# Handing out the recurrences of the first stage: after the ninth projection unit, with RG-LRU one block later and each third's chained parts inside its own group

## The chip, the cores and the metric

The kernel runs on one core of one Trainium2 chip. The metric is the device time of one execution in microseconds, the median of several runs. Three runs of the kernel before gave 2967.48, 2968.40 and 2978.37 us.

## What is computed

One layer of a streaming encoder over T = 2064 tokens (2048 and 16 learned ones in front), width 1024, in float32. Three head groups read one normalised input through one combined projection; their outputs go through one output projection, and a gated feed-forward part follows.

```python
p = rms_norm(h, norm_mix_pre[l]) @ w_in[l]                   # 1024 -> 3080 columns
oa = rg_lru_group(xa, ya, ...)                               # p[:512]: conv, gates, linear recurrence
ob = forgetting_attention_group(q, k, v, f_logit, f_bias)    # p[512:2056]: 8 heads, causal, decay by cumsum(log f)
oc = rwkv7_group(pc, ...)                                    # p[2056:]: 4 heads, 64 x 64 state per head
mixed = jnp.concatenate([oa, ob, oc], axis=-1) @ w_out[l]
h = h + rms_norm(mixed, norm_mix_post[l])
f = causal_dwconv(rms_norm(h, norm_ffn_pre[l]) @ ffn_up[l], ffn_conv[l])
gate, val = jnp.split(f, 2, axis=-1)
h = h + rms_norm((jax.nn.gelu(gate) * val) @ ffn_down[l], norm_ffn_post[l])

def step(S, inp):                                            # the RWKV recurrence, over all tokens
    s_kk = einsum('bhij,bhj->bhi', S, kk_t)
    S = S * w_t[:, :, None, :] - s_kk[..., None] * (kk_t * a_t)[:, :, None, :] + v_t[..., None] * k_t[:, :, None, :]
    return S, einsum('bhij,bhj->bhi', S, r_t)
```

## The kernel before

The program has stages: input projection with the two recurrent groups beside it, attention, output projection, feed-forward up and down. The change is in the first stage only.

**Input projection.** The tokens are worked through in three "thirds" (`part` 0, 1, 2), each of two token blocks (400 and 384, then 384 and 384, then 256 and 256 tokens). For a third, `w_in_part` (L307) is a generator over 25 units, each of 128 output columns: first the gate unit of the attention (`w_in_gate`), then eight units c0 to c7 (the RWKV columns), four a0 to a3 (the RG-LRU columns), and k0 to k3, v0 to v3, q0 to q3. It yields after every unit and token block, in all 50 times for a third, with True where a unit is whole; the last two units, q2 and q3, are interleaved by token block. A unit's matmuls (L177 to L179, PSUM tile `psp`) split each product in three for precision. Columns c and a are stored to a scratch tensor in DRAM (`scr_p`), from which the recurrences load them.

**Recurrences.** RWKV is cut into nine blocks of 256 tokens (the last has 64), three to a third. `Rwkv.block(b)` (L1047) is a generator. Its first part mixes neighbouring tokens, computes decays and gates (matmuls into the one-buffer PSUM tile `eps`, L1075 the first of them), the scores inside a chunk of 64 tokens (L1149, L1154), transposes (L1185), and inverts small triangular matrices on VectorE and GpSimd (L1204, L1205), by way of two DRAM tensors `da` and `dx`; it has four plain yields and then yields `SOLVED`. Its second part ("chained part", ten yields) multiplies the inverses together (L1234, L1278, L1289), carries the 64 x 64 states from chunk to chunk and block to block (L1330, L1334), normalises, and stores to `scr_mix` (L1390 is its last matmul before the store). Its matmuls go to the PSUM tile `rps`, which has two buffers, handed round in program order. `lru_block` (L1453, four yields) does one block of RG-LRU; its state goes from block to block too. `gate_block` (two calls a third) sums the forget gates for attention.

**The order.** `recurrences` (L2113) chains these generators for a third. Per block: the first part up to `SOLVED`; then `R.ending`, which is the chained part of the block before; then this block's RG-LRU. Its own chained part becomes `R.ending` and so comes behind the next block's first part, for the last block of a third in the next third's group, for the very last in the loop behind `beside.finish()`. `Beside` (L2083) holds such groups in a queue and hands out one piece (from one yield to the next) at a time: `advance` is called at every yield of the projection and adds `PACE` = 1.25 to what is due, as long as there is a group; a group begins only when the one before it is at its end. A third's group is added when the unit numbered `READY + 1` = 14 is whole, that is k0, in every third; in the first third the units up to 13 are handed out before the loop begins. What is left after the last third is handed out by `beside.finish()` without projection steps between.

The order in which the program hands out its instructions is a priority: the builder (`schedule_with_timeline_sim=True`) fills each engine's queue, and among instructions that could go at a moment the one handed out earlier goes first. Each engine then works through its queue in that order. Buffers of a tag are handed round in program order.

**Behind it.** The recurrences' pools (`rec`: `ps_rw`, `ps_ae`, `gp`, `rp`) are closed; attention (`Attn.run`) goes through 8 heads with the first half of the queries (two blocks of 512), then 8 heads with the second half. Each of these 32 steps ends with one L761. Some attention tiles (the third key tile `k2_2`, prepared by L499) lie on the side of the memory on which the recurrences' pools were. Only when the first half is through does the output projection begin to run beside attention.

## Time and profile before

| | us |
|---|---|
| median of three runs | 2968.4 |
| the profiled execution | 2975.7 |
| its span, first to last instruction | 2974.0 |
| TensorE matmul busy in the span | 2852.4 (96%) |
| VectorE busy | 2039.5 (69%) |
| ScalarE busy | 1503.8 (51%) |
| GpSimd busy | 1285.9 (43%) |
| mean granted TensorE clock | 0.979 |

The profile is of one execution. The page gives busy times, the span in 40 slices, the DMA queues and the chain of work that ended last; the trace behind it can be asked for the busy time in any stretch, for waits, for groups of instructions by line, and for the instructions in order of time. Times in the trace are counted from the first instruction. "PE" is TensorE's matmuls, "PEld" its weight loads, "DVE" VectorE, "ACT" ScalarE, "POOL" GpSimd, "SP" SyncE, which issues nearly all DMAs. A matmul's end is modelled, so small gaps between matmuls do not show as idle time.

### The profile page before, as it was taken

How to read it: one execution, taken by the hardware profiler on the slowest of the kernel's cores; microseconds unless marked ns; L12 is line 12 of the kernel's file. 1: busy time of each engine (PE TensorE's matmuls, PEld its weight loads, DVE VectorE, ACT ScalarE, POOL GpSimd, SP SyncE). 2: the span in 40 equal slices, each digit the busy share in tenths (PEclk: the TensorE clock that was granted, in tenths of full speed). 3: DMA queues.
4: the chain of work that ended last, by engine and by line, in shares of the span. 5: the costliest groups of instructions: out<-in, count | busy, mean ns of one | idle time of the engine just before them, and what ended most of it. 6: DMA issues, size and time to landing. Idle time of an engine off the chain costs nothing.

```text
span 2974.0 us, 53306 instructions
## 1 busy us (share of the span) xinstructions
PE 2852.4 (96%) x18826; PEld 2444.3 (82%) x18826; DVE 2039.5 (69%) x3977; ACT 1503.8 (51%) x2937; POOL 1285.9 (43%) x1555
## 2 busy tenths in 40 slices
PE   6999999999988889999999999999999999999998
PEld 6998899888866555666568999999999999787887
DVE  5257754665677775566656998888778787646766
ACT  4246432554346655455644665666565665324333
POOL 1001121132114566667722667455655444646443
PEclk9999899999988999999999999999999999999999
DMA  6776479576653358445245665577777764436453
GB/s 216 237 231 220 144 250 320 182 245 218 217 125 81 88 116 229 106 98 136 64 130 189 203 193 175 165 230 211 208 211 219 218 198 138 150 114 221 146 173 121
DMA packets 470344, 530.52 MB, mean 178 GB/s; under 512 B 86862, under 2 KB 356888, under 8 KB 468524
## 3 DMA queue, kind: packets, MB, share of 16 engines
q1 hardware_dynamic: 469308, 526.18, 58.8%
q8 instruction: 148, 2.42, 0.3%
q14 instruction: 120, 0.98, 0.1%
q0 software_dynamic: 768, 0.93, 0.1%
HBM read 368.07 MB, written 158.90 MB: 177 GB/s over the span
## 4 chain that ended last, share of the span: by engine, by line
PE 75%; DVE 8%; DMA 7%; ACT 4%; issue 2%; POOL 2%; SPq 1%; DVEq 0%; POOLq 0%; ACTq 0%
PE psu L177 9%; PE psu L178 9%; PE psu L179 9%; PE psp L179 4%; PE psp L178 4%; PE psp L177 4%; PE psd L177 4%; PE psd L178 4%; PE psd L179 4%; PE po L727 4%; PE pswo L177 2%; PE pswo L178 2%; PE pswo L179 2%; PE sc L704 2%; PE mx L576 2%
## 5 line engine op out<-in xcount | busy, mean ns | idle before, releaser
L178 PE MATMUL psu<-xo,uw 128*128 128x344 f32 x1848 | 591.5, 320 | 0.0
L177 PE MATMUL psu<-xo,uw 128*128 128x344 f32 x1848 | 586.2, 322 | 2.4 <-DVE vb L1889 1.9
L179 PE MATMUL psu<-xo,uw 128*128 128x344 f32 x1848 | 582.0, 320 | 0.3 <-DVE uw L1698 0.3
L177 PE MATMUL psp<-xh,wh 128*128 128x384 f32 (+2 forms) x1152 | 378.7, 329 | 1.4 <-DMA wh<-scr_wk 1.0
L179 PE MATMUL psp<-xh,wl 128*128 128x384 f32 (+2 forms) x1152 | 376.8, 328 | 0.6 <-DMA wl<-scr_wk 0.6
L178 PE MATMUL psp<-xl,wh 128*128 128x384 f32 (+2 forms) x1152 | 375.3, 326 | 0.0
L1698 DVE TENSOR_TENSOR uw<-uq,uw 128x512 fp32r<-128x512 f32 x341 | 320.2, 944 | 59.1 <-ACT uw L1697 55.9
L177 PEld LDWEIGHTS psu<-xo,uw 128*128 128x128 f32 x1848 | 345.9, 188 | 4.2 <-DVE vb L1889 3.0
L178 PEld LDWEIGHTS psu<-xo,uw 128*128 128x128 f32 x1848 | 347.2, 188 | 0.0
L179 PEld LDWEIGHTS psu<-xo,uw 128*128 128x128 f32 x1848 | 345.7, 188 | 1.1 <-DVE uw L1698 1.1
L1697 ACT ACTIVATE uw<-uq 128x512 fp32r<-128x512 f32 x462 | 288.1, 627 | 94.8 <-PE psu L179 44.9
L709 ACT ACTIVATE p<-sc,bias 128x512 f32<-128x512 f32 (+4 forms) x352 | 197.5, 589 | 172.1 <-PE sc L705 142.1
L581 DVE TENSOR_REDUCE mc<-mx 128x1 f32<-128x512 f32 (+6 forms) x352 | 190.7, 567 | 116.7 <-PE mx L576 77.5
L1837 DVE SCALAR_TENSOR_TENSOR uy<-psu,ffn_cols,uy 128x342 f32<-128x342 f32 (+1 forms) x390 | 220.9, 568 | 60.3 <-ACT uy L1835 58.6
L1845 POOL TENSOR_TENSOR uy<-uy,uy 128x342 f32<-128x342 f32 (+1 forms) x132 | 145.1, 1099 | 232.5 <-DVE uy L1837 61.0
L1698 POOL TENSOR_TENSOR uw<-uq,uw 128x512 fp32r<-128x512 f32 x121 | 183.1, 1513 | 133.3 <-ACT uw L1697 111.9
L179 PEld LDWEIGHTS psp<-xh,wl 128*128 128x128 f32 x1152 | 218.6, 190 | 8.9 <-issue 6.2
L177 PEld LDWEIGHTS psp<-xh,wh 128*128 128x128 f32 x1152 | 218.4, 190 | 8.4 <-issue 4.4
L178 PEld LDWEIGHTS psp<-xl,wh 128*128 128x128 f32 x1152 | 218.3, 189 | 7.2 <-issue 5.7
L748 POOL TENSOR_TENSOR acc<-acc,p 128x512 f32<-128x512 f32 (+3 forms) x186 | 198.8, 1071 | 46.8 <-ACT p L709 21.3
L1698 DVE TENSOR_TENSOR fo<-u,fo 128x896 fp32r<-128x896 f32 x88 | 101.6, 1154 | 130.9 <-ACT fo L1697 130.3
L1697 ACT ACTIVATE fo<-u 128x896 fp32r<-128x896 f32 x88 | 81.3, 923 | 207.1 <-PE psd L179 116.0
(490 smaller groups left out, 6339.4 us busy)
## 6 DMA issues: line engine op xcount, KB each, us to landing
uq<-scr_us SPq DMA_DIRECT2D x220, 256.0 KB
uq<-in_ffn_up_dram SPq DMA_DIRECT2D x209, 256.0 KB
wl<-scr_wk SPq DMA_DIRECT2D x48, 512.0 KB
wh<-scr_wk SPq DMA_DIRECT2D x48, 512.0 KB
u<-scr_ff SPq DMA_DIRECT2D x88, 256.0 KB
scr_ff<-uy SPq DMA_DIRECT2D x110, 171.0 KB
raw<-in_w_in_dram SPq DMA_DIRECT2D x24, 512.0 KB
scr_wk<-wh SPq DMA_DIRECT2D x24, 512.0 KB
```

Of the source, the lines that this page charges most:

```text
L177: nc.tensor.matmul(out, ah, bh, start=first, stop=False, skip_group_check=more)
L178: nc.tensor.matmul(out, ah, bl, start=False, stop=False, skip_group_check=more)
L179: nc.tensor.matmul(out, al, bh, start=False, stop=last, skip_group_check=more)
L576: nc.tensor.matmul(ps[:rows, : e - a], q3[:, qo : qo + rows], k2[:, a:e], start=True, stop=not last)
L581: self.reduced = nc.vector.tensor_reduce(mc[:rows, i, ci : ci + 1], ps[:rows, : e - a], axis=AX.X, op=ALU.max)
L709: last = nc.scalar.activation(p[:rows, :w], ps[:rows, :w], AF.Exp, bias=bias[:rows, j : j + 1])
L727: mm = nc.tensor.matmul(po[at : at + 64, c0:n], v1[:rows, j], p[:rows, : n - c0], start=start and i < 2, stop=end and i + 2 >= len(group), ...
L748: eng.tensor_tensor(a, ps_[0][0][:rows, c0:n] if start and i == 1 else a, p[:rows, : n - c0], op=ALU.add)
L1697: core.nc.scalar.activation(hi, src, AF.Copy)
L1698: (eng or core.nc.vector).tensor_tensor(lo, src, hi, op=ALU.subtract)
L1837: core.conved = stt(y[:, :n], src[:, i : n + i], cw[:, 44 * i + cc : 44 * i + cc + 1], y[:, :n], op0=ALU.mult, op1=ALU.add)
L1845: core.pooled = nc.gpsimd.tensor_tensor(v[:, :n], g[:, :n], v[:, :n], op=ALU.mult)
```

## The change

Three things move in program order; no instruction is added or removed.

1. In the second and third thirds the group is added when unit 9 (`ROWS`: the gate unit and c0 to c7) is whole instead of unit 14. The first third is unchanged: k0.
2. A block's RG-LRU comes one block later: behind the first part of the next block, just ahead of the block's own chained part. Before an RG-LRU, pieces are passed over while unit 13 (`READY`) of this third is not whole yet (`R.made`).
3. The chained part of a third's last block, and its RG-LRU, stand at the end of this third's own group instead of inside the next third's, and the loop over `R.ending` behind `beside.finish()` is gone.

```diff
-READY = 13
+READY, ROWS = 13, 9
...
-    for b in ((0, 1, 2), (3, 4, 5), (6, 7, 8))[part]:
+    def rest(b):
+        while R.made < (part, READY):
+            yield
+        yield from lru_block(core, R, scr, lk, b)
+        yield from R.ending
+
+    bs = ((0, 1, 2), (3, 4, 5), (6, 7, 8))[part]
+    for b in bs:
         gen = R.block(b)
         while next(gen) != R.SOLVED:
             yield
-        yield from R.ending
+        if b > bs[0]:
+            yield from rest(b - 1)
         R.ending = gen
-        yield from lru_block(core, R, scr, lk, b)
+    yield from rest(bs[-1])
...
                 for whole in units:
-                    if whole and i == READY + 1:
+                    if whole:
+                        R.made = part, i
+                    if whole and i == (ROWS if part else READY + 1):
                         beside.add(recurrences(core, R, lk, a["fox_f_bias"], scr, blocks, part))
                     beside.advance()
...
         beside.finish()
-        for _ in R.ending:
-            pass
         rec.close()
```

So the order of one third is, before: gates; first part b, chained part b-1, RG-LRU b; first part b+1, chained part b, RG-LRU b+1; and so on. After: gates; first parts b and b+1; RG-LRU b, chained part b; first part b+2; RG-LRU b+1, chained part b+1; RG-LRU b+2, chained part b+2.

## The prediction

> **What bounds the kernel now.** The page first: its engine line, the slices and the chain that ended last.
>
> ```profile
> PE 2852.4 (96%) x18826; PEld 2444.3 (82%) x18826; DVE 2039.5 (69%) x3977; ACT 1503.8 (51%) x2937; POOL 1285.9 (43%) x1555
> PE   6999999999988889999999999999999999999998
> PEclk9999899999988999999999999999999999999999
> PE 75%; DVE 8%; DMA 7%; ACT 4%; issue 2%; POOL 2%; SPq 1%; DVEq 0%; POOLq 0%; ACTq 0%
> ```
>
> TensorE is the bound nearly everywhere. Only slices 12 to 15 (a slice is 2974.0 / 40 = 74.4 us, so 818 to 1115 us) have it below nine tenths, with a lower granted clock in two of them. So the second view is the busy time by stretch, around that place:
>
> ```profile
> core 0: us, PE busy (x) PEld busy (x) DVE busy (x) ACT busy (x) POOL busy (x), PEclk, DMA share, GB/s
> 440.00:500.00 60.00, 59.34 (x361) 55.97 (x358) 26.25 (x60) 17.53 (x37) 10.82 (x14) 1.00 0.93 315
> 700.00:855.00 155.00, 148.95 (x1725) 136.17 (x1726) 101.57 (x279) 80.51 (x172) 31.23 (x57) 0.99 0.61 192
> 855.00:875.00 20.00, 11.76 (x99) 8.29 (x98) 17.58 (x46) 2.59 (x8) 0.59 (x2) 0.71 0.44 113
> 875.00:920.00 45.00, 40.48 (x262) 28.18 (x262) 34.13 (x92) 25.22 (x57) 14.05 (x24) 0.75 0.70 149
> 920.00:1040.00 120.00, 104.61 (x1262) 70.78 (x1261) 93.46 (x276) 73.39 (x165) 67.76 (x115) 0.89 0.33 79
> 1040.00:1080.00 40.00, 36.85 (x285) 22.48 (x284) 30.37 (x76) 23.74 (x53) 26.16 (x39) 1.00 0.53 128
> 1080.00:1120.00 40.00, 31.31 (x142) 18.36 (x143) 27.73 (x76) 18.45 (x38) 25.60 (x37) 0.87 0.50 112
> 855.00:1136.00 281.00, 238.28 (x2116) 155.21 (x2115) 211.22 (x578) 152.08 (x335) 142.81 (x229) 0.87 0.47 108
> 1200.00:1400.00 200.00, 198.36 (x907) 127.47 (x905) 118.09 (x249) 100.50 (x187) 134.72 (x193) 0.99 0.44 106
> ```
>
> The projections keep TensorE full (148.95 of 155 us), and so does attention once the output projection fills its holes (198.36 of 200). Between them, 855 to 1136 us, stands the "bridge": 281.00 - 238.28 = 42.7 us of idle TensorE. What fills the bridge is told by the third view, instructions in order of time:
>
> ```profile
> 565.47 0.70 PE L1075 MATMUL eps<-rwwa,wa_up 64*128 64x256 f32 x2
> 613.71 0.39 PE L296 MATMUL psf<-xh,fw 128*128 128x256 f32 x1
> 766.91 1.13 PE L1075 MATMUL eps<-rwwa,wa_up 64*128 64x256 f32 x4
> 833.12 1.13 PE L1075 MATMUL eps<-rwwa,wa_up 64*128 64x256 f32 x4
> 847.73 1.15 PE L1278 MATMUL rps<-rww,rwsc 64*64 64x64 f32 x32
> 855.24 0.28 PE L179 MATMUL psp<-xh,wl 128*128 128x256 f32 x1
> 926.74 0.66 PE L1075 MATMUL eps<-rwwa,wa_up 64*128 64x64 f32 x4
> 1034.18 0.59 ACT L761 ACTIVATE oh<-po 64x512 f32<-64x512 f32 x1
> 1091.89 0.43 PE L1390 MATMUL rps<-rwsg,g_up 128*128 128x64 f32 x2
> 1102.38 0.59 ACT L761 ACTIVATE oh<-po 64x512 f32<-64x512 f32 x1
> 1135.62 0.60 ACT L761 ACTIVATE oh<-po 64x512 f32<-64x512 f32 x1 [1.89 <-PE po L727]
> ```
>
> The last projection matmul is at 855.24. RWKV still runs: block 5's chained part has just begun (L1278, 847.73), block 7's first part too (L1075, 833.12), block 8 starts at 926.74, and the last block ends at 1091.89. The first half of attention (16 steps, each ended by an L761) ends at 1135.62. How much RWKV and RG-LRU matmul lies on either side of 855, by their two PSUM tiles (rps first, then eps):
>
> ```profile
> 100.00:855.00 755.00, 143.49 (x3016) 115.11 (x3016) 71.15 (x162) 56.42 (x138) 0.98 0.68 220
> 855.00:1100.00 245.00, 66.93 (x1278) 53.18 (x1278) 33.17 (x91) 20.02 (x52) 0.87 0.45 105
> 100.00:855.00 755.00, 64.41 (x223) 34.06 (x223) 23.04 (x56) 27.35 (x66) 0.98 0.68 220
> 855.00:1100.00 245.00, 10.14 (x40) 5.93 (x40) 4.01 (x11) 4.14 (x12) 0.87 0.45 105
> ```
>
> 66.93 + 10.14 = 77.1 us of it run in the bridge.
>
> **The change, part by part.** No instruction is added or removed; matmuls, DMAs and waits per block stay. Only the places in program order move, so the cost is a matter of what TensorE does in which stretch.
>
> *Where the pieces land.* `Beside` takes 1.25 pieces per projection step, and a third has 50 steps (2 of the gate unit, 48 of the others). I count pieces in both orders: gates 2, a block's first part 4 to its SOLVED mark, its chained part 10, RG-LRU 4. Before, block 4 starts at the second step of q0, block 6 at k1's second step, block 7 at q0's second, and 39 pieces are left to `finish`. After, the second third starts its gates not at the ninth unit but at a2, because the first third's pieces (ten more, with block 2's chained part) must run out first; it ends in c7 of the last third, that third's ninth unit. There block 6 starts at a0, block 7 at a2, block 6's chained part at k1, block 8 at v1, block 7's chained part at q0; 15 pieces are left over, and all but one belong to block 8, a quarter of a block. `made` holds nothing up: the thirteenth unit is handed out before either third's first RG-LRU.
>
> *Does time follow place?* Block 4's L1075 at 565.47 falls in q0 to q1 of its third, where its piece is handed out, and block 6's 766.91 some 15 us behind its k1. So it follows, with a lag. But places become later in time, as more stands before them: the second third hands out 62.5 pieces instead of 46 (50 x 1.25, against 17 left from the first third and 23 x 1.25). A whole block's piece is worth 1.9 us (next paragraph), so the last third starts some 31 us later, at 645 instead of 613.71. A step of it takes (855.24 - 613.71) / 50 = 4.8 us; a0 is its 19th, so 645 + 92 + 15 = about 750 for block 6 (767 before). Block 7 follows it by at least the 833.12 - 766.91 = 66 us seen between them, about 818 (833), and block 8 by as much again, about 884 (927). Only block 8, and the chained parts, move by more than a few steps.
>
> *What leaves the bridge.* In whole-block pieces, before: chained parts of 5 and 6 (20), 16 of block 7 with its RG-LRU, block 8 at a quarter of 18 (4.5): 40.5 for 77.1 us, 1.9 each. After, by place: block 7's chained part (10), its RG-LRU (4), block 8 (4.5): 18.5, and 42 us moved. But block 6's chained part stands behind block 7's first part, about 818 + 66 = 884, so by the latency most of it is left too, 28.5 and 23 us moved. I take 26, near the latency end since the times above are near it: **27.6 us of matmul move ahead of the last projection**, which ends near 883. By itself this gives nothing: in 700 to 855 TensorE is full, and the work only changes sides.
>
> *What the bridge then costs.* Its TensorE work falls from 238.3 to 238.3 - 27.6 = 210.7 us. Its first 65 us keep their idle time (8.24 + 4.52 = 12.8 us for 52.2 of work: attention has to load its first keys). Then RWKV's rest runs to about 1049, if it takes the 1091.89 - 926.74 = 165 us from block 8's start that it takes now, with the same pieces left: from 948 that is 101 us at the rate of 920 to 1040, 15.39 idle per 104.61, so 13.0 idle and 88.0 of work. The other 70.5 us of work need an idle rate that the trace shows only for other mixtures. Bounds: 1.64 per 198.4 (1200 to 1400, with output projection) and 8.69 per 31.31 (1080 to 1120). I take 3.15 per 36.85 (1040 to 1080, attention with the last of RWKV, the nearest), 6.0 us. So the idle time falls from 42.7 to 31.8: **-10.9 us**. The ends: with 42 us moved and the best rate for all behind the hand-over, 12.8 + 144.2 x 0.0083 = 14.0, so -28.7; with the worst rate for all of that, 12.8 + 40.0, so +10.1.
>
> *A wait that goes.* The 1080 to 1120 row is not typical of attention alone; the chain there says why:
>
> ```profile
> 1094.89 3.29 DVE k L499 x4
> 1098.97 0.47 SPq L539
> 1099.49 4.40 DMA k<-scr_cl
> ```
>
> The third key tile lies where RWKV's tiles were; it is prepared as soon as the last block is done (1092 to 1095), and the second half's maxima wait for it. With RWKV over near 1049, some 40 us ahead of it, that wait is gone. It is in the rate above, not added.
>
> *What it costs the projections.* A projection matmul behind a recurrence's in TensorE's queue stands behind its wait too. First an unmixed stretch (60 to 120 us) against a mixed one (360 to 440), then the waits of 420 to 855 us, then those of the bridge:
>
> ```profile
> L177 PE MATMUL psp<-xh,wh 128*128 128x384 f32 (+1 forms) x113 | 38.4, 340 | 0.0
> L177 PE MATMUL psp<-xh,wh 128*128 128x384 f32 x104 | 36.5, 351 | 1.0 <-DMA wh<-scr_wk 1.0
> PE rps L1234 <- DVE rwxu L1250: 3.4, 3, 1.4
> PE rps L1310 <- ACT rww L1294: 5.9, 3, 3.0
> PE rps L1330 <- DVE rstate L1334: 4.4, 1, 4.4
> PE sc L704 <- ACT p L709: 9.8, 10, 2.0
> PE mx L576 <- DVE mc L581: 8.7, 10, 3.7
> ```
>
> Beside RWKV a projection matmul takes 351 for 340 ns. Ahead of 855 the two tiles have 143.49 + 64.41 = 207.9 us in 755, so 27.6 us more mean some 100 us of mixed stretch, with 3 x 104 x 100 / 80 = 390 projection matmuls: 0 to 390 x 11 ns = 4.3 us, and I take 2, half. The DMA side is busiest where block 2's chained part now falls (share 0.93 in 440 to 500); its small loads there are hidden as long as the weight waits stay at the 1.0 us above.
>
> *Clock.* It is 0.89 in 920 to 1040, 0.71 and 0.75 just after the gap at 855. Between 0 and (1 - 0.89) x 120 = 13 us are in it; I take 1, since the stretched matmuls stand in the busy time of both sums and the dip behind the hand-over stays. [...]
>
> Sum: -10.9 + 2 - 1 = **-9.9 us**. The profiled execution took 2975.7 us (span 2974.0), 0.25% over the median of 2968.4, so the sum is set against the median: **2958.5, or 2958 us**.
>
> **The rivals.** They need one more row, attention's first matmul in the chain:
>
> ```profile
> 873.70 1.10 PE sc L704 x2
> ```
>
> 1. *Nothing gained (2967, between 2964 and 2977).* The bridge's idle time is attention's own. For it: the two largest waits of the bridge, 9.8 and 8.7 us, are scores behind exponentials and maxima behind reductions. Then the rate stays near 15.39 per 104.61, 23.3 us for the 158.5 us behind the first 65; a saving of 6.6, less 2 to 4, and more idle time still where the rate of 1080 to 1120 stays. Against: with RWKV beside them four heads took (1034.18 - 873.70) / 4 = 40.1 us each, three heads from there to 1102.38 took 22.7.
> 2. *Slower (2991).* RWKV is the filler of the bridge's holes. In 855 to 875 the two tiles hold most of the 11.76 busy us (attention begins at 873.70). If the pieces left over wait for one another at the hand-over and that fill is gone, the gap grows by up to 10 us; with the worst rate behind it, (40.0 + 12.8 + 10) - 42.7 + 3 = +23 us. It turns slower where the idle time behind the hand-over exceeds (42.7 - 12.8) / 158.5, 6.3 in 40 us.
> 3. *More gained (2942).* Time follows place throughout: 42 us move, RWKV is over near 980, and the rate of 1040 to 1080 holds for the 144.2 us of work behind the first 65, 12.3 us: 25.1 of idle time, -17.6; with half of the clock's 13 and a better rate up to -32. Taken: -26. For it: the 565.47 row, where place alone set the time.
> 4. *It doesn't move.* If latency alone sets RWKV's pace, the blocks stay where they are and the time at 2968; that is part of rival 1's chance.
>
> **How the numbers follow.** About 0.5% (14.8 us) is what a measurement of this kernel tells from no change. Forecast 0.38 (2949 to 2964), rival 1 with 4 0.25, slower 0.15 (a fifth of it within 0.5%), more gained 0.22 (2930 to 2949). Faster by over 0.5%, under 2953.6: 0.22 + 0.16 of the forecast + 0.02 of rival 1 = 0.40. Slower: 0.12. Same: 0.48. The forecast's own range is 2949 to 2964. The range, 2933 to 2978, takes in nearly all of rival 3 and the +10.1 of the worst rate, and leaves out most of rival 2.
>
> **What would show it.** L1075 of blocks 6, 7 and 8 near 750, 818 and 884, the last L1390 near 1049, the last projection matmul near 883, the 16th L761 near 1125. In the busy time by stretch: TensorE still over 95% in the last third, some 32 us of idle between the last projection and the 16th L761, no chain through L499 to L539. Wrong, if the projections end later by clearly more than the matmul that moved (stalls in the queue), or if heads without RWKV take over 27 us; more gained, if block 8 starts ahead of 860.

## The result, and the profile after

| | before | after |
|---|---|---|
| median | 2971.8 us (4 runs, 2967.5 to 2978.4) | 2996.9 us (4 runs, 2994.1 to 2998.7) |
| ratio, 95% interval | | 1.0082 [1.0059, 1.0105] |
| the profiled execution, its span | 2975.7, 2974.0 | 2998.7, 2996.9 |
| mean granted clock | 0.979 | 0.973 |

The changed kernel is slower by 25 us, outside the range of the prediction (2933 to 2978). The page of after, its engine line, slices and chain:

```profile
PE 2860.5 (95%) x18826; PEld 2448.8 (82%) x18826; DVE 2040.3 (68%) x3977; ACT 1507.5 (50%) x2937; POOL 1291.2 (43%) x1555
PE   7999999998988889999999999999999999999998
PEclk8999899999987899999999999999999999999999
PE 75%; DVE 8%; DMA 5%; ACT 5%; POOL 3%; issue 3%; SPq 1%; DVEq 0%; POOLq 0%; ACTq 0%
```

The same instructions (x18826 on TensorE in both) keep TensorE busy 8 us longer, and the span is 23 us longer, so two thirds of the loss are idle time of TensorE (in a second pair of traces, runs 9 and 10 below, 9 us of 21). The busy time by stretch tells where; first two rows of before, then after, cut at the gate units of the thirds, the last projection matmul, the 16th and the 32nd L761 (columns: length, then busy time of PE, PEld, DVE, ACT, POOL, then clock, DMA share, GB/s):

```profile
315.00:614.00 299.00, 293.68 (x2516) 266.00 (x2515) 173.00 (x433) 113.17 (x222) 57.02 (x87) 1.00 0.71 234
614.00:855.00 241.00, 230.70 (x2679) 209.37 (x2679) 154.74 (x411) 117.70 (x252) 55.81 (x96) 0.99 0.65 206
```

```profile
316.00:642.00 326.00, 313.30 (x2831) 282.29 (x2828) 202.01 (x503) 139.61 (x276) 66.39 (x104) 0.98 0.70 229
642.00:876.00 234.00, 222.63 (x2500) 204.54 (x2501) 134.15 (x353) 94.23 (x202) 44.22 (x71) 0.98 0.61 193
876.00:1155.00 279.00, 232.26 (x1949) 149.22 (x1948) 213.47 (x578) 160.10 (x345) 146.94 (x233) 0.85 0.45 109
1155.00:1543.00 388.00, 375.80 (x1727) 222.35 (x1724) 231.73 (x470) 204.31 (x371) 250.78 (x340) 0.99 0.45 118
1543.00:2997.00 1454.00, 1431.10 (x8000) 1325.74 (x8000) 1082.78 (x1597) 775.40 (x1496) 749.92 (x737) 1.00 0.59 184
```

The second third takes 27 us more, the last third 7 less, and the bridge only 2 less (281 before). Behind the bridge the two are within 4 us. So the question is what the second third got for its 27 us. The two tiles of the recurrences in after, for the three thirds and the bridge (rps first, then eps; columns: length, busy time, clock, DMA share, GB/s):

```profile
36.00:316.00 280.00, 30.18 (x448) 0.96 0.66 214
316.00:642.00 326.00, 67.38 (x1500) 0.98 0.70 229
642.00:876.00 234.00, 57.92 (x1240) 0.98 0.61 193
876.00:1155.00 279.00, 56.08 (x1110) 0.85 0.45 109
```

```profile
36.00:316.00 280.00, 19.31 (x66) 0.96 0.66 214
316.00:642.00 326.00, 26.12 (x88) 0.98 0.70 229
642.00:876.00 234.00, 16.79 (x61) 0.98 0.61 193
876.00:1155.00 279.00, 14.36 (x48) 0.85 0.45 109
```

Ahead of the last projection now lie 217.7 us of recurrence matmul (before 207.9), in the bridge 70.4 (before 77.1). So some 7 to 10 us moved, not 27.6; the last projection nevertheless ends 21 us later (876.4 for 855.5). RWKV itself ends later, not earlier:

```profile
763.77 1.13 PE L1075 MATMUL eps<-rwwa,wa_up 64*128 64x256 f32 x4
794.64 1.13 PE L1075 MATMUL eps<-rwwa,wa_up 64*128 64x256 f32 x4
804.64 1.03 PE L1086 MATMUL eps<-rwsq,gat 128*4 128x256 f32 x4 [0.42 <-ACT rwe L1077]
898.33 1.22 PE L1105 MATMUL eps<-rwix,spr 4*128 4x256 f32 x2
938.14 0.66 PE L1075 MATMUL eps<-rwwa,wa_up 64*128 64x64 f32 x4
1108.66 0.33 PE L1390 MATMUL rps<-rwsg,g_up 128*128 128x64 f32 x2
1154.79 0.59 ACT L761 ACTIVATE oh<-po 64x512 f32<-64x512 f32 x1 [2.07 <-PE po L727]
```

Block 7 starts at 795, 38 us earlier than before, and then its first part stands still from L1086 (804.64) to L1105 (898.33). VectorE's instructions in order of time say why:

```profile
888.88 0.29 DVE L1205 TENSOR_REDUCE rwix<-rwitmp 128x8 f32<-128x128 f32 x1
889.08 0.40 DVE L1088 TENSOR_SCALAR rwia<-eps 4x256 f32<-4x256 f32 x1
```

L1088 writes the tile `rwia`, which has one buffer and is also the scratch of the triangular inversion. It starts 0.2 us after the start of the last L1205 of block 6's inversion. With two first parts in a row, the second one's norms wait for the first one's inversion, and everything behind them in the order waits too. So nothing uses the two `rps` buffers between block 6's last L1185 (872) and block 7's first L1149 (905).

That pause falls on the hand-over to attention. TensorE around the last projection matmul in after:

```profile
876.08 0.28 PE L179 MATMUL psp<-xh,wl 128*128 128x256 f32 x1
885.92 1.10 PE L704 MATMUL sc<-q,k 128*128 128x512 f32 x2 [9.56 <-DMA q<-scr_qh]
```

It does nothing for 9.56 us, until attention's first queries are loaded. Before, block 5's chained part ran at that place (11.76 us busy in the first 20, attention's first matmul at 873.70).

### The profile page after: what moved, and what is told of

Same layout as the page of the kernel before. It is cut to its first block, busy times and chain, and to the rows that moved or that the text cites. A ratio compares the mean times of both kernels' runs of the same rounds, so it can differ in the third digit from the quotient of the medians.

```text
span 2996.9 us, 53351 instructions
## 1 busy us (share of the span) xinstructions
PE 2860.5 (95%) x18826; PEld 2448.8 (82%) x18826; DVE 2040.3 (68%) x3977; ACT 1507.5 (50%) x2937; POOL 1291.2 (43%) x1555
## 4 chain that ended last, share of the span: by engine, by line
PE 75%; DVE 8%; DMA 5%; ACT 5%; POOL 3%; issue 3%; SPq 1%; DVEq 0%; POOLq 0%; ACTq 0%
PE psu L177 9%; PE psu L178 9%; PE psu L179 9%; PE psp L179 4%; PE psp L178 4%; PE psp L177 4%; PE psd L177 4%; PE psd L178 4%; PE psd L179 4%; PE po L727 4%; PE pswo L177 2%; PE pswo L178 2%; PE pswo L179 2%; PE sc L704 2%; PE mx L576 2%
## 5 line engine op out<-in xcount | busy, mean ns | idle before, releaser
L748 POOL TENSOR_TENSOR acc<-acc,p 128x512 f32<-128x512 f32 (+3 forms) x186 | 196.2, 1057 | 52.0 <-ACT p L709 19.4
```

Source lines behind the costliest of these rows:

```text
L748: eng.tensor_tensor(a, ps_[0][0][:rows, c0:n] if start and i == 1 else a, p[:rows, : n - c0], op=ALU.add)
```

## Two theories, and what tells them apart

After these traces two theories were set up, and more came as runs contradicted them. The *chain theory*: RWKV's sections on the two `rps` buffers (first part L1149 to L1185, some 20 us; chained part L1234 to L1390, 60 to 77 us) run one after another in program order; the change fills a 65 us pause of that chain in the second third, but makes two new ones (31 and 34 us), and the time follows RWKV's end. The *load theory*: TensorE is full ahead of the last projection, the bridge's idle time is attention's own, so work moved across the last projection gains nothing and costs over a us for each us moved. From the fifth run on stand beside them a *boundary theory* (the loss is made where the second third passes to the third) and an *order theory* (any other order than that of before costs 10 us or more by chance).

The kernel before took 2981 to 2984 us (median) on the chips of the experiments (runs 1 to 4 and 9 to 12 on one, 5 to 8 on a second, 13 on a third), so each ratio goes by runs of both kernels on its chip. The other columns of a row are of one profiled execution, which can lie well off its kernel's median: run 1's took 2998.4 us for a median of 2991.1, run 9's 2977.8 for 2983.1. Differences named below are from the first trace of before; from run 9, on the chip of runs 1 to 4, those of the last projection are 3.7 us smaller. All numbers of the traces together; "rec" is the busy time of the two tiles as above, "fill" TensorE's busy time in the first 20 us behind the last projection, "rest" is the bridge less its rec less 204.3 us (run 13):

| kernel | ratio, 95% interval | second third | last projection | RWKV's end | 16th L761 | rec ahead | rec in bridge | bridge | fill | rest |
|---|---|---|---|---|---|---|---|---|---|---|
| before, first trace | | 298.8 | 855.5 | 1092.3 | 1136.2 | 207.9 | 77.1 | 280.7 | 11.8 | -0.7 |
| after, first trace | 1.0082 [1.0059, 1.0105] | 325.5 | 876.4 | 1109.0 | 1155.4 | 217.7 | 70.4 | 279.0 | 6.4 | 4.3 |
| 1 after, own scratch | 1.0037 [1.0022, 1.0052] | 335.7 | 901.9 | 1057.1 | 1157.3 | 235.3 | 49.4 | 255.4 | 13.8 | 1.7 |
| 2 before, ninth unit | 1.0057 [1.0042, 1.0072] | 329.2 | 887.1 | 1062.4 | 1158.0 | 231.2 | 57.5 | 270.9 | 8.4 | 9.1 |
| 3 before, RG-LRU later | 1.0059 [1.0039, 1.0078] | 300.8 | 870.1 | 1103.0 | 1159.4 | 214.9 | 72.4 | 289.3 | 7.2 | 12.6 |
| 4 after, unit 14 | 1.0062 [1.0039, 1.0085] | 311.8 | 874.1 | 1120.9 | 1165.9 | 217.5 | 71.5 | 291.8 | 6.9 | 16.0 |
| 5 before, PACE 1.0 | 1.0114 [1.0096, 1.0133] | 308.1 | 858.0 | 1133.0 | 1174.5 | 197.0 | 90.5 | 316.5 | 14.0 | 21.7 |
| 6 last third alone | 1.0028 [1.0014, 1.0041] | 304.2 | 863.2 | 1105.9 | 1149.5 | 209.1 | 71.3 | 286.3 | 6.8 | 10.7 |
| 7 first two thirds alone | 1.0071 [1.0053, 1.0090] | 329.0 | 887.5 | 1106.5 | 1164.9 | 220.1 | 65.9 | 277.4 | 4.1 | 7.2 |
| 8 after, q1 to q3 held | 1.0042 [1.0028, 1.0056] | 325.5 | 877.4 | 1097.5 | 1150.4 | 217.2 | 65.0 | 273.0 | 5.2 | 3.7 |
| 9 before again | 1.0005 [0.9993, 1.0016] | 301.2 | 859.2 | 1094.0 | 1139.2 | 207.3 | 75.8 | 280.0 | 11.8 | -0.1 |
| 10 after again | 1.0053 [1.0040, 1.0067] | 327.2 | 879.3 | 1113.7 | 1158.7 | 218.3 | 71.8 | 279.4 | 6.7 | 3.3 |
| 11 before, own scratch | 1.0009 [0.9997, 1.0021] | 295.9 | 870.9 | 1107.9 | 1147.0 | 211.0 | 71.6 | 276.1 | 10.0 | 0.2 |
| 12 before, PACE 1.5 | 1.0025 [1.0010, 1.0039] | 305.0 | 867.4 | 1098.8 | 1143.1 | 209.7 | 76.7 | 275.7 | 13.1 | -5.3 |
| 13 after without blocks 6 to 8 | 0.9707 [0.9646, 0.9768] | 323.7 | 858.2 | 841.3 | 1062.5 | 199.8 | 0.0 | 204.3 | 8.5 | 0 |

## The experiments

### 1. After, with a scratch of its own for the norms

In the norms of a block's first part:

```diff
-        ks2, kinv, ktmp = (self.t([P, 256], s)[:4, :n] for s in ("ia", "ix", "itmp"))
+        ks2, kinv = (self.t([P, 256], s)[:4, :n] for s in ("ja", "jx"))
+        ktmp = flat(wa[:])[:4]
```

> The changed kernel, with its own scratch for the key norms of a block's first part (two new tags and the used-up wa tile instead of ia, ix, itmp, which the block before still needs for its inversion). Chain theory: RWKV's work on the two rps buffers is one chain, and the changed order puts two first parts in a row twice (blocks 3 and 4, 6 and 7); the second one's norms wait for the first one's inversion, which leaves holes of 31 and 34 us in the chain. Then the holes fall below 12 us each, the last RWKV matmul comes near 1055 instead of 1109, and the time falls from 2997 to 2970 to 2985. Load theory: the time is lost by the projections, which carry more RWKV work earlier and whose thirds begin late; then the holes may close but the time stays at 2992 to 3005, and the projections end no earlier than 876.

The wait is what stops block 7: its L1086 (805.5 in both kernels, to 1 us) is followed by the norms' next matmul at 816.4 instead of 898.3, the two pauses of 31 and 34 us shrink to 5 and 3, and RWKV ends at 1057 instead of 1109. So the chain theory is right about where RWKV runs. About the time it is wrong (2991 us, not 2970 to 2985; the load theory's 2992 to 3005 is missed by 1): with RWKV's end 52 us earlier, the 16th L761 is where it was (1157.3 and 1155.4), in an execution 7 us over the median. The busy time by stretch of this run, last third and bridge:

```profile
653.00:902.00 249.00, 232.59 (x2652) 211.06 (x2650) 160.12 (x427) 115.42 (x250) 51.97 (x92) 0.97 0.63 194
902.00:1157.00 255.00, 213.64 (x1602) 135.43 (x1602) 169.96 (x475) 136.56 (x291) 136.93 (x210) 0.87 0.49 115
```

The bridge has lost 21 us of recurrence matmul and is 24 us shorter; its idle time, 41.4 us, is that of before (42.7) with 28 us less recurrence matmul beside it. The last projection ends 25.5 us later for the 17.6 us that moved ahead of it. This is the load theory's picture. Against run 10 on the same chip the ratio falls from 1.0053 to 1.0037: the wait for `rwia` has a small part in the loss, if any (the intervals overlap).

### 2. Before, with the ninth unit alone

Groups are added at `ROWS` as in the change, with the `R.made` test ahead of an RG-LRU; the order inside a group is that of before.

```diff
-READY = 13
+READY, ROWS = 13, 9
...
+        while R.made < (part, READY):
+            yield
         yield from lru_block(core, R, scr, lk, b)
...
-                    if whole and i == READY + 1:
+                    if whole:
+                        R.made = part, i
+                    if whole and i == (ROWS if part else READY + 1):
```

> The kernel before, in which only the start of the second and third groups moves to the ninth unit (an RG-LRU still waits for the thirteenth); order within a group and the carried-over chained part as before. Chain theory: no two first parts stand in a row, the hole of 65 us between block 1's chained part and block 3's first part shrinks to 15 to 30, all that follows comes 35 to 50 us earlier, the last RWKV matmul near 1050 instead of 1092, the projections end near 870, and the time is 2950 to 2964. Load theory: RWKV is earlier by as much as the changed kernel wanted, so the projections suffer as there: 2985 or more.

No first parts in a row, the 65 us pause of the chain gone, RWKV over at 1062, and as slow as the whole change: 23.3 us more recurrence matmul ahead of the last projection, which ends 31.6 us later, and a bridge that is 10 us shorter for 19.6 us taken out of it.

### 3. Before, with RG-LRU one block later alone

```diff
+        if b % 3:
+            yield from lru_block(core, R, scr, lk, b - 1)
         yield from R.ending
         R.ending = gen
-        yield from lru_block(core, R, scr, lk, b)
+    yield from lru_block(core, R, scr, lk, b)
```

> The kernel before, in which only the RG-LRU comes one block later (ahead of the chained part of its own block, the last one of a third at the end of its group). Chain theory: RG-LRU uses no rps buffer, so the chain, its one hole of 65 us and the time stay: 2962 to 2978. Load theory: nothing is handed out earlier, so the same. Rival: the RG-LRU between first part and chained part delays the chained part on VectorE and ScalarE; then the last RWKV matmul is 10 us or more later than 1092 and the time 2980.

The first two thirds stay as they are (the third gate unit starts at 616.7, before 613.7), and the loss is as large as the whole change's again. The last third takes 253.4 us for 241.8, with 6.7 us more recurrence matmul in it, and the hand-over is emptier: fill 7.2 for 11.8, idle time of the bridge 49.4 us. None of the expectations has this time (2999 us); the rival, which has RWKV's end 10 us later, comes nearest. So runs 2 and 3 say that the parts of the change don't add up: each of these two alone costs what all cost together.

### 4. After, with the group at unit 14

```diff
-                    if whole and i == (ROWS if part else READY + 1):
+                    if whole and i == READY + 1:
```

> The changed kernel with the groups added at the fourteenth unit again, so that the order within and between groups is the only difference from before. Chain theory: in the changed kernel the blocks 3 and 6 were held by the chained parts ahead of them, not by the unit, so starting later changes little in the second third and something in the last: holes of about 30 us between blocks 3 and 4 and 6 and 7 as there, the time 2990 to 3005. Load theory: part of the load is back in its old place, so between the two kernels, 2978 to 2988.

Pauses of 35 and 36 us as in after, RWKV's end at 1121, the bridge 292 us long. The time, 3000 us, is the chain theory's (2990 to 3005) and not the load theory's (2978 to 2988). The early start is not what hurts here; the bridge is longer by 13 us than that of after with the same RWKV in it.

### 5. Before, with fewer pieces: the other direction

```diff
-PACE = 1.25
+PACE = 1.0
```

> The kernel before, with PACE 1.0 instead of 1.25, so that less RWKV is handed out ahead of the last projection: the opposite direction of the change. Load theory (the bridge has 42 to 55 us of TensorE idle time whatever of RWKV lies in it, so moving RWKV across the last projection gains nothing, and every us of it ahead of that point makes the projections end over 1 us later): last projection earlier, some 830 to 845 us instead of 855.5, RWKV before it 155 to 170 us instead of 182, bridge longer by the same, idle of the bridge 40 to 50; ratio 0.993 to 1.000. Filler theory (RWKV's work is worth most as the filler of the bridge): the same direction, ratio under 0.995. Order theory (the order of before is a good one by chance, and any other costs 15 to 25 us in new waits, whichever direction): ratio 1.004 to 1.009.

The load theory, and the theory that RWKV is welcome filler, both said faster; it is the slowest of all, above the order theory's range too. 10.9 us less recurrence matmul ahead of the last projection don't bring it forward (858.0), and 13.4 us more in the bridge make it 36 us longer. The chain of waits of this run, behind RWKV's end at 1133:

```profile
1135.99 1.11 DVE k L499 x3
1138.50 4.05 DMA k<-scr_cl
1142.69 1.31 PE mx L576 x3
```

That is the chain L499 to L539 of the prediction: the third key tile lies where RWKV's tiles were. TensorE's waits in the bridge, the three longest lines:

```profile
PE mx L576 <- DVE mc L581: 17.3, 17, 2.8
PE mx L576 <- DMA k<-scr_cl: 9.7, 1, 9.7
PE sc L704 <- ACT p L709: 7.5, 8, 2.0
```

9.7 us for the key tile, 1.7 in the trace of before. So RWKV's end does bind when it is late enough: the 16th L761 comes 41.5 us behind it here, 43.9 in before; in runs 1 and 2, where RWKV ends early, 96 to 100.

### 6 and 7. The change in the last third alone, and in the first two alone

Run 6 has the group at `ROWS` and the new order in the last third only; run 7 in the first two only, with the loop over `R.ending` kept.

```diff
-        if b > bs[0]:
-            yield from rest(b - 1)
+        if part < 2 or b == bs[0]:
+            yield from R.ending
+        else:
+            yield from rest(b - 1)
         R.ending = gen
-    yield from rest(bs[-1])
+        if part < 2:
+            yield from lru_block(core, R, scr, lk, b)
+    if part == 2:
+        yield from rest(bs[-1])
...
-                    if whole and i == (ROWS if part else READY + 1):
+                    if whole and i == (ROWS if part == 2 else READY + 1):
```

> The change in the last third alone; the first two as before (block 5's chained part comes behind block 6's first part as before). Boundary theory (most of the loss is made where the second third passes to the third: more RWKV is handed out there, and the next third's norm stands behind it on VectorE and ScalarE): the third third starts near 614 as before, the last projection ends within 5 us of 855.5 plus the RWKV matmul that moves ahead of it, ratio 0.998 to 1.002. Load theory: the gain in the bridge is nothing, and the RWKV matmul that moves ahead of the last projection (some 10 to 20 us) makes it late by more, ratio 1.001 to 1.004. Order theory: 1.004 to 1.009.

> The change in the first two thirds alone; the last third as before (group at unit 14, RG-LRU right behind the first part, block 8's chained part behind the queue). Boundary theory: nearly the whole loss, the third third starts at 635 to 645 instead of 613.7, idle time of the second third 11 to 14 us instead of 5.3; ratio 1.005 to 1.008. Load theory: more RWKV ahead of the third third (81 us instead of 65), the same behind; the last projection ends later by that and RWKV ends earlier than 1092; ratio 1.002 to 1.006. Order theory: 1.004 to 1.009.

The last third alone costs about half of what the whole change costs in run 10 (another chip), with next to no recurrence matmul moved; its loss shows in the bridge (fill 6.8, rest 10.7), and 1.0028 is the load theory's range and not the boundary theory's. The first two thirds alone cost all of it: 12.2 us moved ahead of the last projection, which ends 32 us later, and an almost empty hand-over (fill 4.1). Run 7's ratio is where the boundary theory put it, and its third gate unit at 647.2, 2 us past the range; the order theory has this ratio too. What the boundary theory gives as the cause is the next run's question.

### 8. After, with nothing handed out in the second third's last six steps

```diff
-                    beside.advance()
+                    if part != 1 or i < 23:
+                        beside.advance()
```

> The changed kernel, with nothing handed out from the recurrences during the last four steps (q2, q3) of the second third's projection. Boundary theory: the gap between the last matmul of q3 and the first of the third third's gate unit falls from 15.8 us to some 4, the third third starts 8 to 12 us earlier than 641.8 beside what RWKV moves behind it, and the time falls by 8 to 12 us, ratio 1.003 to 1.006 over the kernel before. Load theory: a part of the same (the 15.8 us are partly filled by RWKV), 0 to 8 us, ratio 1.004 to 1.009. If the gap stays near 15 us, the norm is not late by what is handed out in q2 and q3.

The edit holds back six steps and not four: `i` is 23 while q1 is made, so q1 hands out nothing either. The gap between q3's last matmul and the third gate unit stays: 16.3 us, 15.8 in after, 3.8 in before. In the trace of after, TensorE and VectorE in that gap:

```profile
632.45 0.44 PE L145 MATMUL pst<-ident,xt 128*128 128x128 f32 x2
636.87 2.11 PE L145 MATMUL pst<-ident,xt 128*128 128x128 f32 x8 [3.98 <-DVE xl L152]
641.80 0.58 PE L296 MATMUL psf<-xh,fw 128*128 128x256 f32 x1
```

```profile
630.25 0.68 DVE L152 TENSOR_TENSOR xl<-pst,xh 128x512 fp32r<-128x512 f32 x1
...
631.71 0.29 DVE L1205 TENSOR_REDUCE rwix<-rwitmp 128x8 f32<-128x128 f32 x1
632.03 1.72 DVE L1257 TENSOR_TENSOR rwxf<-rps,rwxu 32x256 f32<-32x256 f32 x4
633.78 0.41 DVE L1088 TENSOR_SCALAR rwia<-eps 4x256 f32<-4x256 f32 x1
...
636.12 0.68 DVE L152 TENSOR_TENSOR xl<-pst,xh 128x512 fp32r<-128x512 f32 x1
```

In after the next third's norm (L152) shares VectorE with the end of block 4's inversion, block 3's chained part and block 5's first part, and TensorE waits 3.98 us for it. By the count of pieces these were handed out ahead of q1, or nearly so, and the same lines stand in the gap of run 8, with a wait of 4.53 us; holding the last steps back doesn't touch them. Its ratio, 1.0042, is below the 1.0053 of run 10 (on another chip; the intervals overlap). What its trace has over run 10's is the clock: the bridges of run 10 and run 8 hold the same 1956 matmuls, 1158 of them the recurrences'.

```profile
879.00:1159.00 280.00, 231.65 (x1956) 151.91 (x1956) 210.88 (x580) 160.42 (x346) 145.49 (x231) 0.85 0.46 109
877.00:1150.00 273.00, 223.94 (x1956) 142.84 (x1955) 215.17 (x573) 159.71 (x346) 146.43 (x227) 0.90 0.47 111
```

In run 8 they took 7.7 us less, at a granted clock of 0.90 for 0.85, and the 6.8 us less recurrence matmul in the table are part of that, not work that moved. The gap as the boundary theory's cause was not removed by this run, and its price stays open.

### 9 and 10. Both kernels again

> The kernel before, unchanged, for a trace on the chip of the runs beside it (its median there was 2981 to 2982 us where the first profile's was 2975.7). Order theory and boundary theory alike: span some 2978 to 2984, the extra 5 to 9 us over the first trace spread over the stages; if they lie in the second third (298.8 us in the first trace), a part of what the experiments showed there belongs to the chip and not to the order.

> The changed kernel on the chip of the runs beside it. If the loss belongs to the order: ratio 1.006 to 1.010 as at first, the third third's gate unit 20 us or more later than in the kernel before on the same chip. If it belongs to the chip or to the run: ratio 1.000 to 1.004.

On one chip the stages differ as in the first pair: third gate unit +30.1 us, last projection +20.1, 16th L761 +19.5, span +21.1 (2976.1 and 2997.2). The loss belongs to the order, though its ratio there, 1.0053, lies between the two ranges: the changed kernel's median is nearly the first one (2998.8 for 2996.9), the kernel before's is 11 us higher (2983.0 for 2971.8). By the medians the loss is 16 us; the traces show 21, since run 9's is 5 us below its median.

### 11. Before, with the scratch of its own

The edit of run 1 on the kernel before.

> The kernel before with the scratch of the norms of a block's first part apart from that of the triangular inversion (as in the first experiment, on the other kernel). The rings' sections of the kernel before have no gap that this wait makes but the 65 us in the second third, which waits for the hand-out. Chain theory: same, 0.998 to 1.001. Order theory: the fill of the engines' queues shifts all the same, and any shift costs 10 us or more: 1.003 to 1.007. If it is under 0.998, the wait for that scratch costs the kernel before too, and this beats both.

Against run 9 its stages shift by up to 9 us (the first and last thirds longer, the second shorter), and the time is that of before within the interval. So the order theory in its strong form falls: a shifted order doesn't cost 10 us by itself. The hand-over is filled here (10.0).

### 12. Before, with more pieces

`PACE = 1.5`.

> The kernel before with PACE 1.5 instead of 1.25; with 1.0 the ratio was 1.0114. Order theory: slower too, 1.003 to 1.010, with more idle time of TensorE ahead of the last projection. Load theory turned round (the more RWKV is ahead of the last projection the better, and the change loses by its RG-LRU place alone): faster, 0.990 to 0.998, RWKV's end before 1080 us.

Slower, by a quarter of what PACE 1.0 cost; the load theory turned round said faster. RWKV ends at 1099 (1094 in run 9), not earlier: the sections follow one another, and more pieces a step didn't bring their end forward. The bridge is the best of all for its load (rest -5.3, fill 13.1), and the last projection is 8 us later than in run 9 for 2.4 us more recurrence matmul ahead of it.

### 13. After, without the recurrences of blocks 6 to 8

```diff
-    bs = ((0, 1, 2), (3, 4, 5), (6, 7, 8))[part]
+    bs = ((0, 1, 2), (3, 4, 5), ())[part]
...
-    yield from rest(bs[-1])
+    if bs:
+        yield from rest(bs[-1])
...
+                    for r in (0, 768):
+                        nc.gpsimd.dma_start(scr["mix"][r : r + 256, 1488:T], x[0:256, 0 : T - 1488])
```

> The changed kernel without RWKV and RG-LRU of blocks 6 to 8 (their rows of the mixed tensor are filled from the input instead), so that no recurrence is left in the bridge and next to none in the last third. Attention's pace (the bridge's idle time is attention's own, whatever runs beside it): idle time between the last projection and the 16th L761 40 to 50 us, as in every kernel so far (38 to 60), the bridge 205 to 220 us long, 60 to 75 shorter than the changed kernel's 279, about the recurrence matmul taken out (63 us) and no more. Recurrences make the idle time (their waits hold up attention in TensorE's queue): idle 12 to 25 us, bridge 180 to 195 us. For the last third: with TensorE full, its 234 us should fall by the 65 us of recurrence matmul and, if mixing costs more than the matmul itself, by some 75 to 80.

The last third and the bridge of this run, and TensorE's longest waits in that bridge:

```profile
642.00:858.00 216.00, 207.90 (x2505) 194.80 (x2503) 112.74 (x304) 72.02 (x148) 38.90 (x61) 0.99 0.66 203
858.00:1062.00 204.00, 165.71 (x783) 96.09 (x783) 103.74 (x258) 100.55 (x207) 123.14 (x187) 0.88 0.57 132
```

```profile
PE sc L704 <- DMA q<-scr_qh: 10.2, 1, 10.2
PE mx L576 <- DVE mc L581: 9.0, 15, 2.4
PE sc L704 <- ACT p L709: 7.8, 8, 3.4
```

With no recurrence in it the bridge has 204.00 - 165.71 = 38.3 us of idle time, against 42.7 in before and 46.7 in after. These 38.3 us are attention's own: its first load, its maxima and its exponentials. So on balance the recurrences fill none of it; with them it is 4 to 8 us more. Sorted by the matmul that ended each pause, before's 42.7 us are 28.3 ahead of attention's matmuls and 14.4 ahead of recurrence matmuls (the prediction's lines for L1310 and L1330, 5.9 and 4.4, are the largest of them); in run 1 they are 28.9 and 12.4, in run 10 35.9 and 12.5. So with recurrences beside attention the idle time is not all attention's: they cover up to 10 us of its pauses, mostly the first load (0.9 us of waiting in before, 10.2 here), and bring 12 to 14 of their own.

The last third is 17.6 us shorter than in run 10 and the bridge 75.1; run 10 has 86 us more of recurrence matmul there, 14.2 in the last third and 71.8 in the bridge. That makes 1.05 us for each in the bridge and 1.24 in the last third, by one execution of each kernel on two chips; 3 us more or less, as between the two traces of before, would make the second price 1.0 to 1.5. The last third did not fall by the 65 us expected, since 61.8 us of the recurrences of blocks 3 to 5 still ran in it. This is the load theory's picture: a us of recurrence matmul is worth about one us in the bridge, and one or somewhat more beside the projections. It does not account for runs 4 and 5.

## Why the prediction was wrong

- **What bounds the kernel: right.** TensorE, with the bridge as the one stretch with idle time. The last third kept its 95% (222.63 of 234).
- **Where the pieces land: right for two starts, wrong for what follows them.** L1075 of blocks 6 and 7 came at 764 and 795 (750 and 818 said), block 8's at 938 (884). Order and latency were weighed, but not the tiles that two first parts share: block 7's stood 94 us inside itself, where `rwia` held it. With a tile of its own it stood 11 (run 1), which shows that wait as the cause.
- **What leaves the bridge: mis-sized.** 27.6 us said, 7 (out of the bridge) to 10 (ahead of the last projection) measured. The last L1390 came at 1109, not 1049. That the last projection came near the 883 said (876) is chance: 9.8 us had moved ahead of it and 11 were added, for 27.6 and 2 in the sum.
- **What the bridge then costs: this is the step that failed.** It gave idle time a rate by the mixture beside which it was seen, lower with less RWKV, and so a saving of 10.9 us. Measured, it rose by 4 (to 46.7), and run 1, with 28 us less recurrence matmul in the bridge than before, still had 41.4, run 13 with none 38.3. A right forecast of how much moves would not have saved this term: run 1 took 27.7 us out of the bridge, and the time rose. Nor did the parts of the idle time follow the amount: ahead of attention's matmuls it is 28.9 us in run 1 and 28.3 in before, ahead of recurrence matmuls 12.4 and 14.4.
- **The first 65 us of the bridge: not kept.** They were said to keep their 12.8 us of idle time. In after the first 20 us are 6.4 busy instead of 11.8, because the pause for `rwia` emptied the hand-over. That is rival 2's mechanism, at a smaller price than its 10 us. Run 1 fills the hand-over again (13.8), and "rest", the part of the bridge that neither attention alone nor rec explains, falls from 4.3 to 1.7.
- **The wait that goes (L499 to L539): it left the chain without a gain.** In after the third key tile is prepared at 1111.86, right behind RWKV's end as before; the chain of waits at that place runs by the sums' way through DRAM (DMA scr_rden, then rb) instead. Run 5 shows the same wait at 9.7 us where RWKV ends at 1133: it bounds how late RWKV may end, not how early.
- **What it costs the projections: mis-sized, and the larger part of the loss.** 0 to 4.3 us was said, by matmuls of 351 for 340 ns. That rate held: a projection matmul of the second third has a median of 338 ns in after, 337 in before. What it left out is, first, idle time: TensorE stood idle 8.5 us more ahead of the last projection (54.7 for 46.2) in the first pair of traces, 3.8 more (55.0 for 51.2) in runs 9 and 10. The part that repeats is the second third's, 7.4 and 6.6, of it 4 in the one wait at the boundary of the thirds (run 8). Second, the other matmuls were busy 2.7 us longer, 5.2 in the second pair, with the granted clock of the second third 0.02 lower in both. So the last projection came 21 us later for 9.8 us of matmul, which the prediction had named as a sign of being wrong. Why the surplus is as large as it is (2 to 16 us over run 9 in the orders tried, and not in step with the amount moved) stays open; run 8 was meant to tell and missed its object.
- **The clock: 1 us of gain said, a lower clock measured.** 0.98 for 1.00 in the second third, 0.85 for 0.87 in the bridge (0.97 for 0.99 and 0.85 for 0.88 in runs 10 and 9). In the first 20 us from 876 on, which hold the 9.56 us of nothing, the clock was 0.63 (0.70 before), and 0.71 in the 45 that follow (0.75). The gap alone doesn't set it: run 1, whose longest pause in its first 20 us is 2.4, has 0.65 there, and run 8, idle for 14.8 of its first 20 us and at 0.55 in them, has 0.90 over the whole bridge, so the 0.02 of the bridge is not clear of what executions differ by.
- **The rivals.** Rival 1 had the outcome in the bridge, no gain, and half of the mechanism: attention alone has 38.3 us of idle time (run 13), but before's is not all attention's. Its time of 2967 left the projections' price at 2 to 4 us. Rival 2 had the sign and one of the places. Its other half, RWKV as a filler on balance, is refuted by run 13: without RWKV there is less idle time, not more. Rival 3 fails with the forecast, since time did not follow place. Rival 4, the blocks stay where they are, is near for RWKV (block 6 at 764 for 767, the end 17 us later) and wrong about the time.

The sum as measured, from the third gate marks, 16th L761 and tiles of the first pair: second third +26.7 us (19.0 of them recurrence matmul moved in), last third -7.2 (9.6 moved out), bridge -1.7 (6.7 moved out), the first third with what precedes it +1.3; together +19.2 at the 16th L761, and +3.7 behind it. Of the 33 us between the forecast's -9.9 and the measured +22.9 of the spans, 15 are the bridge's idle time (+4.0 for -10.9) and 9 the projections (+11 for +2).

No order tried beats the kernel before; the nearest is run 11, the same within its interval. The table suggests why, and no run tests it: before keeps the hand-over filled (11.8) and RWKV's end some 44 us ahead of the end of attention's first half, where the third key tile is hardly waited for (1.7 us), and leaves as little as that allows beside the projections.

## What to carry to other kernels

A stretch of idle time next to a movable piece of work is not yet room for that work or relief from it: take the piece out altogether once and see whether the idle time goes (run 13; 38 us stayed, of 43 in before and 48 in run 10). Moving work from a stretch with idle time into one where the bound engine is full gains only if the idle time goes with it; here it never did (42.7 us in before, 46.7 in after, 41.4 in run 1), and moving work the other way (run 5, 1.0114) lost more. When two instances of a section are put next to each other, look first for single-buffered scratch that they share (`rwia` held block 7's first part for 94 us; with a tile of its own it stood 11); and look at what the moved work covered where it was, here the 10 us of attention's first loads.

## What was not expected of the hardware

- Between the last projection and attention's first scores TensorE waits about 10 us for the first load of queries (9.56 us in after, where that load is issued at 881.43, 5 us into the wait, and 10.2 in run 13) when no other matmul runs there; in before, where block 5's chained part runs there, the wait is 0.9. The clock is 0.62 to 0.63 in the 20 us with that gap in both. In runs 7 and 8 TensorE is idle for 15.95 and 14.79 of the first 20 us, at a clock of 0.57 and 0.55.
- The median of the kernel before differed by 10 to 13 us between the first runs (2971.8) and those on three chips later (2981 to 2984), half the size of the effect, and the changed kernel's by 2 (2996.9 and 2998.8), while the profiled spans of the two kernels repeated to 2.1 and 0.3 us (2974.0 and 2976.1, 2996.9 and 2997.2). Whether the chip makes the difference isn't shown, since the chip of the first runs is not on record. Stages of two traces of one kernel differ by up to some 4 us: the last projection of before is at 855.5 in one trace and 859.2 in the other.
